# Nine gathers of the second layer placed between chunks made ahead, and the tokens' rows of h built before the top-k

## The chip, the cores and the metric

One core of a Trainium2 chip runs the whole program. The metric is the device time in microseconds, taken as the median of three runs: 3376.2 us before (3373.15 to 3382.22). One more execution was recorded by the hardware profiler; all rows below come from it.

## The reference

The program is two networks one after the other. The first has two layers, and each layer ends in a PEER block, a feed-forward layer with 16384 experts of which each token uses 8 heads times 16:

```python
q = (xc @ wq).reshape(C, PEER_HEADS, 2, PEER_KEY_DIM)
s = jnp.einsum('chpd,hpnd->chpn', q, sub_keys).astype(jnp.float32)
s1, i1 = lax.top_k(s[:, :, 0], PEER_TOPK)
s2, i2 = lax.top_k(s[:, :, 1], PEER_TOPK)
cand = (s1[..., :, None] + s2[..., None, :]).reshape(C, PEER_HEADS, PEER_TOPK * PEER_TOPK)
...
top, pos = lax.top_k(cand, PEER_TOPK)
eidx = jnp.take_along_axis(cidx, pos, axis=-1)
g = jax.nn.softmax(top, axis=-1).astype(xc.dtype)
a = jax.nn.gelu(jnp.einsum('chkd,cd->chk', u_tab[eidx], xc))
return jnp.einsum('chk,chkd->cd', g * a, v_tab[eidx])
```

The first layer's block runs over 512 tokens (latents and context), the second's over the 256 latents. The second network follows and is not touched.

## The kernel before

`peer` (from L707 on) computes the block in two ways at once. The first TD tokens (320 in the first layer, 192 in the second) go through all 16384 experts densely, in 128 chunks of 128 experts: TensorE multiplies the chunk's u rows (`peer_uT`) with h, ScalarE takes the gelu into a tile G (`expert_in`), VectorE multiplies G by the chunk's routing weights (A, L823), A is split into a high and a low part (Ahl, L128 and L129), and TensorE accumulates Ahl times the chunk's v rows (`peer_v`; lines L186 to L188 and L856, tiles ps). The remaining tokens, 64 in the second layer, are served by gathering: 64 indirect DMAs (L925, POOL's queue), each of which brings 128 pairs of u and v rows into a tile gat of 128 x 2048 floats, some 1.05 MB; there are four such tiles. For each gather VectorE multiplies u with the token's row of h and sums (L928), ScalarE applies gelu and the weight (L929, L930), and VectorE adds the weighted v row to gacc (L942; the first is L940). The gather of four places later can start when that has read its tile.

The order of one block is: norm and scores; the top-k of all heads on VectorE (`best`); `route`, which turns the result into indices (idx) for the gathers and into dense weights that POOL writes to DRAM (wd, L1065, twelve DMAs in the second layer); then the chunks made ahead, `AHEAD` of them (30 in the second layer, all with whole fp32 matmuls, L883, which need neither VectorE nor routing weights); then the main loop, which loads the routing weights of eight chunks at a time (win, L820, on POOL's queue, which reads wd) and runs chunk c's A while TensorE accumulates the v of chunk c - 3. From chunk 30 on the loop also makes its own u. The gathers are started by the generator `gathered`: each `next` issues one gather. In the first layer six are begun between the chunks made ahead (`if both and c % 2`), in the second none; the loop at L832 spreads the rest evenly over the chunks.

Before its first gather, `gathered` makes h2: the 64 tokens' rows of h, token by partition, by eight additions of the high and low part of h (hs, L919), eight transposes on TensorE (L920) and two copies (L921).

Instructions are put in order per engine by a scheduler at build time and run in that order on the chip: an instruction that waits holds all behind it on its engine, and a DMA that waits holds its queue. The loads of u and v (raw, L136) go over SP's queue into a ring of five tiles; each load starts when the tile five places earlier has been used. Up to four loads ahead are held split (whi, wlo).

Of the kernel before, what the change touches and what calls it, by code (L numbers as in the profile page):

```python
# [9 lines left out]
F32 = mybir.dt.float32  # L10
# [9 lines left out]
D = 1024  # L20
# [20 lines left out]
def bc(ap, shape):  # L41
    return ap.to_broadcast(shape)
# [6 lines left out]
class Net:  # L49
# [660 lines left out]
    def peer(self, l, both):  # L710


        nc, i = self.nc, self.i
        NT = 4 if both else 2
        T, TD = NT * 128, DENSE[l]
        nd, part = TD // 128, TD % 128
        assert part in (0, 64)
        ng = (T - TD) * 128 // 128
        xt, modT = self.xt, self.modT
        with ExitStack() as es:  # L720
            pa = self.pool(es, f"pa{l}")
            lp = self.pool(es, f"lp{l}")

            h2 = pa.tile([128, 8, 2, T], FR, name="h2hl")
            hT = h2[:, :, 0], h2[:, :, 1]
            h32 = None if both else pa.tile([128, 8, T], F32, name="h2f")
            sc = self.mod_scale(modT, 4, "nfT", l, pa)
            idx = pa.tile([128, max(ng, 1)], I32, name="idx")
            gg = pa.tile([128, max(ng, 1)], F32, name="gg")
# [12 lines left out]
            pos = [vp.tile([128, 8, 16], U32, name=f"pos{t}") for t in range(NT)]  # L742
            with ExitStack() as e2:
                np_ = self.pool(e2, "wqp", side="right")
                scs = {}

                def scores(cg):

                    qT = np_.tile([128, 4, 512], F32, tag="pq", name="pq", bufs=2)
                    keys = np_.tile([128, 4, 128], F32, tag="keys", name="keys", bufs=2)  # L750
                    nc.gpsimd.dma_start(keys, i["keysT"][l, cg])
                    for c in range(4):
                        ps = self.psum(c % 2)
                        self.proj_T(ps[:, :T], hT, i["wq"][l, cg * 4 + c], 0, T)
                        nc.scalar.copy(qT[:, c, :T], ps[:, :T])
                        yield
                    for t in range(NT):
                        ps = self.psum()
                        for k in range(4):
                            nc.tensor.matmul(ps[:, k * 128:k * 128 + 128], qT[:, k, t * 128:t * 128 + 128], keys[:, k],  # L760
                                             start=True, stop=True)
                        sc = scs[cg, t] = np_.tile([128, 512], F32, tag="score", name="score", bufs=8)
                        nc.scalar.copy(sc, ps)

                def best(cg):
                    for t in range(NT):
                        sc = scs[cg, t]
                        for c in range(4):
                            n = cg * 4 + c
                            self.top16(np_, sc[:, c * 128:c * 128 + 128], v16[t][:, n], i16[t][:, n], "tk")  # L770
                        self.candidates(np_, v16[t], top[t], pos[t], cg)


                made = [scores(cg) for cg in range(4)]
                for cg in range(5):
                    if cg < 4:
                        next(made[cg])
                    if cg:
                        for _ in made[cg - 1]:
                            pass  # L780
                    for _ in range(3 if cg < 4 else 0):
                        next(made[cg])
                    if cg and both:
                        best(cg - 1)
                if not both:
                    for cg in range(4):
                        best(cg)
            with ExitStack() as e2:
# [13 lines left out]
            ahead = AHEAD[l]  # L802
            em.close()
            gp = self.pool(es, f"gp{l}", side="right")
            gat = self.gathered(gp, hT, idx, gg, TD, T) if ng else iter(())

            gs, g0 = [], 0
            for c in range(ahead):
                gs.append(self.expert_in(lp, l, c, h2, h32, TD, c < WHOLE[l]))
                if both and c % 2:  # L810
                    next(gat, None)
                    g0 += 1
            acc = [[self.psum(t == 2 and n) for n in range(2)] for t in range(nd + bool(part))]
# [3 lines left out]
            for c in range(128):  # L817
# [4 lines left out]
                a = gp.tile([128, TD], F32, tag="A", name="A", bufs=2)  # L822
# [35 lines left out]
            for t in [*range(nd + bool(part), NT), *range(nd + bool(part))]:  # L858
                oo = gp.tile([128, 2, D], F32, tag="gat", name="gat", bufs=4)
                for n in range(2):  # L860
                    d = slice(n * 512, n * 512 + 512)
                    o, ps = oo[:, 0, d], acc[t][n] if t <= nd and t * 128 < TD else None
                    if t == nd and part:
                        self.evac(oo[:, 1, d], ps)
                        ps = self.psum()
# [35 lines left out]
        nc.scalar.activation(g, src, AF.Gelu_apprx_tanh)  # L901
        return g

    def gathered(self, gp, hT, idx, gg, t0, t1):


        nc, i = self.nc, self.i
        self.gacc = {}
        s0, prev = 0, None
        for t in reversed(range(t0 // 128, t1 // 128)):  # L910
            b = max(t0, t * 128)
            w = t * 128 + 128 - b
            h2 = gp.tile([128, D], F32, tag="h2", name="h2", bufs=1)
            for n in range(2):
                ps = self.psum(True)
                for k in range(4):
                    hs = gp.tile([128, 128 // w, w], F32, tag="hs", name="hs", bufs=2)
                    hh, hl = (bc(x[:, n * 4 + k, None, b:b + w].bitcast(F32), [128, 128 // w, w]) for x in hT)
                    nc.vector.tensor_add(hs, hh, hl)  # L919
                    nc.tensor.transpose(ps[:, k * 128:k * 128 + 128], hs.rearrange("p a b -> p (a b)"), self.ident)  # L920
                nc.scalar.copy(h2[:, n * 512:n * 512 + 512], ps)  # L921
            acc = self.gacc[t] = gp.tile([128, D], F32, tag="gacc", name="gacc", bufs=2)
            for s in range(s0, s0 + w):
                uv = gp.tile([128, 2, D], F32, tag="gat", name="gat", bufs=4)
                nc.gpsimd.indirect_dma_start(out=uv.rearrange("p a b -> p (a b)"), out_offset=None, in_=i["peer_uv"],  # L925
                                             in_offset=bass.IndirectOffsetOnAxis(ap=idx[:, s:s + 1], axis=0))
                a = gp.tile([128, 2], F32, tag="pga", name="pga", bufs=4)
                nc.vector.scalar_tensor_tensor(uv[:, 0], uv[:, 0], 1.0, h2, op0=OP.mult, op1=OP.mult, accum_out=a[:, 0:1])  # L928
                nc.scalar.activation(a[:, 1:2], a[:, 0:1], AF.Gelu_apprx_tanh)  # L929
                nc.scalar.activation(a[:, 1:2], a[:, 1:2], AF.Copy, scale=gg[:, s:s + 1])  # L930
                if prev:
                    self.gather_add(*prev)
                prev = acc, uv, a, s == s0
                yield
            s0 += w
        self.gather_add(*prev)
# [784 lines left out]
```

## Time and profile before

| | |
|---|---|
| median of the timed runs | 3376.2 us |
| profiled execution, its own time | 3371.84 us |
| its span | 3370.1 us |
| PE busy | 3230.3 us (96%) |
| DVE busy | 2607.3 us (77%) |
| ACT busy | 1748.3 us (52%) |
| POOL busy | 519.6 us (15%) |
| DMA | 860.52 MB, mean 255 GB/s |

The time of the profiled execution is 1.7 us over its span, and 4.4 us under the median of the timed runs. PE being busy 96% of the span is a mean over many stages. The second layer's PEER block takes the stretch from about 1957 to 2700 us; its top-k and routing lie between 1982 and 2146 us, and its main loop from 2161 us on.

### The profile page before, as it was taken

The page shows a single profiled execution, that of the slowest core. Times are in us where ns is not written, and L with a number is a line of the kernel's source. Part 1 is how long each engine was busy: PE and PEld are TensorE (multiplying, and loading weights), DVE is VectorE, ACT ScalarE, POOL GpSimd, SP SyncE. Part 2 cuts the span into 40 slices and gives each one's busy share as a digit, 9 for nine tenths or more (in the row PEclk, how much of TensorE's full clock was granted, in tenths as well). Part 3 has the DMA queues.
Part 4 walks back from the last instruction along what each step waited for, and adds up shares of the span by engine and source line. Part 5 has one row for each costly group of instructions (what it writes and reads, how often), then busy time and mean ns, then how long its engine had stood idle before and what let it go on. Part 6 is the DMA issues. An engine that isn't in the chain of part 4 may idle for free. (4 is left out here: it accounts for less than half of the span.)

```text
span 3370.1 us, 53059 instructions
## 1 busy us (share of the span) xinstructions
PE 3230.3 (96%) x19449; PEld 2775.4 (82%) x19449; DVE 2607.3 (77%) x5430; ACT 1748.3 (52%) x3720; POOL 519.6 (15%) x432
## 2 busy tenths in 40 slices
PE   8999999879899999999999997989999999999998
PEld 5666788758788989888877997769999988889887
DVE  3643449998899999999966678599999968756875
ACT  3443332385455555554545544557777755555554
POOL 0000000113333333333300000122222100000000
PEclk9999999879999999999999998999999999999999
DMA  6566232569999999999944555889999854255432
GB/s 243 187 213 225 85 125 83 167 185 345 375 400 391 387 388 388 380 393 386 377 166 163 179 179 174 286 347 384 367 377 377 336 173 157 94 185 177 137 126 107
DMA packets 196453, 860.52 MB, mean 255 GB/s; under 512 B 23920, under 2 KB 25664, under 8 KB 159712
## 3 DMA queue, kind: packets, MB, share of 16 engines
q1 hardware_dynamic: 141840, 505.94, 41.6%
q0 software_dynamic: 54352, 351.20, 27.1%
q8 instruction: 153, 2.51, 0.3%
q14 instruction: 108, 0.88, 0.1%
HBM read 816.15 MB, written 40.89 MB: 254 GB/s over the span
## 5 line engine op out<-in xcount | busy, mean ns | idle before, releaser
L129 DVE TENSOR_TENSOR wlo<-raw,whi 128x1024 fp32r<-128x1024 f32 x778 | 943.9, 1221 | 392.7 <-ACT whi L128 379.9
L128 ACT CAST whi<-raw 128x1024 fp32r<-128x1024 f32 x778 | 815.8, 1049 | 627.2 <-PE pf L187 247.4
L925 POOL DMA_INDIRECT gat<-peer_uv,idx x256 | 413.8, 1616 | 918.8 <-DVE gacc L942 875.2
L188 PE MATMUL pf<-h2hl,wlo 128*128 128x320 f32 (+2 forms) x1152 | 361.9, 314 | 7.6 <-DVE wlo L129 7.6
L186 PE MATMUL pf<-h2hl,whi 128*128 128x320 f32 (+2 forms) x1152 | 362.7, 315 | 0.2 <-ACT mo L321 0.2
L187 PE MATMUL pf<-h2hl,whi 128*128 128x320 f32 (+2 forms) x1152 | 361.8, 314 | 0.0
L928 DVE SCALAR_TENSOR_TENSOR gat<-gat,h 128x1024 f32<-128x1024 f32 x256 | 312.1, 1219 | 32.5 <-DMA gat<-peer_uv,idx 31.2
L942 DVE SCALAR_TENSOR_TENSOR gacc<-gat,pga,gacc 128x1024 f32<-128x1024 f32 x253 | 323.5, 1279 | 0.0
L187 PE MATMUL ps<-wlo,Ahl 128*128 128x512 f32 x768 | 305.4, 398 | 10.5 <-DVE wlo L129 10.4
L186 PE MATMUL ps<-whi,Ahl 128*128 128x512 f32 x768 | 302.3, 397 | 2.8 <-ACT Ahl L128 2.8
L188 PE MATMUL ps<-whi,Ahl 128*128 128x512 f32 x768 | 303.4, 395 | 0.5 <-DVE Ahl L129 0.5
L892 PE MATMUL pf<-h2hl,whi 128*128 128x384 f32 x784 | 238.3, 359 | 4.6 <-ACT whi L128 4.3
L188 PEld LDWEIGHTS pf<-h2hl,wlo 128*128 128x128 f32 x1152 | 217.9, 189 | 11.6 <-DVE wlo L129 8.8
L187 PEld LDWEIGHTS pf<-h2hl,whi 128*128 128x128 f32 x1152 | 218.2, 189 | 8.0
L186 PEld LDWEIGHTS pf<-h2hl,whi 128*128 128x128 f32 x1152 | 218.2, 189 | 7.8 <-ACT mo L321 0.3
L128 ACT CAST Ahl<-A 128x320 fp32r<-128x320 f32 (+1 forms) x256 | 103.7, 405 | 164.2 <-DVE A L823 158.0
L187 PEld LDWEIGHTS ps<-wlo,Ahl 128*128 128x128 f32 x768 | 145.0, 189 | 37.5 <-DVE wlo L129 14.0
L891 PE MATMUL pf<-h2hl,wlo 128*128 128x192 f32 x686 | 174.9, 255 | 0.0
L188 PEld LDWEIGHTS ps<-whi,Ahl 128*128 128x128 f32 x768 | 145.3, 189 | 34.9 <-DVE Ahl L129 1.0
L186 PEld LDWEIGHTS ps<-whi,Ahl 128*128 128x128 f32 x768 | 145.0, 189 | 28.6 <-ACT Ahl L128 4.1
L892 PEld LDWEIGHTS pf<-h2hl,whi 128*128 128x128 f32 x784 | 147.5, 188 | 9.4 <-ACT whi L128 5.2
L856 PE MATMUL ps<-wlo,Ahl 128*128 128x512 f32 x384 | 151.4, 397 | 0.0
(613 smaller groups left out, 7574.7 us busy)
## 6 DMA issues: line engine op xcount, KB each, us to landing
raw<-peer_uT SPq DMA_DIRECT2D x256, 512.0 KB
raw<-peer_v SPq DMA_DIRECT2D x256, 512.0 KB
raw<-ada_w SPq DMA_DIRECT2D x96, 512.0 KB
wd<-wb POOLq DMA_DIRECT2D x32, 1024.0 KB
raw<-w_g SPq DMA_DIRECT2D x48, 512.0 KB
win<-wd POOLq DMA_DIRECT2D x16, 1280.0 KB
raw<-wq SPq DMA_DIRECT2D x32, 512.0 KB
raw<-w2o SPq DMA_DIRECT2D x32, 512.0 KB
```

What stands on the lines that cost most here:

```text
L128: nc.scalar.copy(hi, src)
L129: nc.vector.tensor_sub(lo, src, hi.bitcast(F32))
L186: mm(ps, ah, bh, start=start, stop=False)
L187: mm(ps, ah, bl, start=False, stop=False)
L188: self.last = mm(ps, al, bh, start=False, stop=stop).ins
L856: nc.tensor.matmul(acc[nd][n], ahl[:, 2 * TD - part:], v[e][:, n], start=b == 0 and e == 0, stop=b == 127 and e == 1)
L891: mm(src, u[1][:, k], h2[:, k, 0, :TD], start=False, stop=False)
L892: self.last = mm(r3(ps[:, :2 * TD], 2), u[0][:, k], h2[:, k, :, :TD], start=k == 0, stop=k == 7).ins
L925: nc.gpsimd.indirect_dma_start(out=uv.rearrange("p a b -> p (a b)"), out_offset=None, in_=i["peer_uv"], in_offset=bass.IndirectOffsetOnAxi ...
L928: nc.vector.scalar_tensor_tensor(uv[:, 0], uv[:, 0], 1.0, h2, op0=OP.mult, op1=OP.mult, accum_out=a[:, 0:1])
L942: self.nc.vector.scalar_tensor_tensor(acc, uv[:, 1], a[:, 1:2], acc, op0=OP.mult, op1=OP.add)
```

## The change

Three edits, all in the PEER block of the second layer:

- The code that makes h2 becomes a function `by_token`, which the second layer calls before `best`, in the pool lp. `gathered` takes the ready tile. The first layer still makes it inside `gathered`.
- Between the chunks made ahead, `gathered` is now also stepped in the second layer, after chunks 13, 15, ... 29: nine gathers.
- With nine done, the loop spreads 55 gathers over its chunks instead of 64, by the same rule.

```diff
@@ peer @@
                 np_ = self.pool(e2, "wqp", side="right")
-                scs = {}
+                scs, h2s = {}, {}
...
                 if not both:
+                    h2s[nd] = self.by_token(lp, hT, TD, part)
                     for cg in range(4):
                         best(cg)
...
-            gat = self.gathered(gp, hT, idx, gg, TD, T) if ng else iter(())
+            gat = self.gathered(gp, hT, idx, gg, TD, T, h2s) if ng else iter(())
...
                 gs.append(self.expert_in(lp, l, c, h2, h32, TD, c < WHOLE[l]))
-                if both and c % 2:
+                if c % 2 and (both or c > 11):
                     next(gat, None)
                     g0 += 1
@@ new, with the body that stood in gathered @@
+    def by_token(self, gp, hT, b, w):
+        nc = self.nc
+        h2 = gp.tile([128, D], F32, tag="h2", name="h2", bufs=1)
+        for n in range(2):
+            ps = self.psum(True)
+            for k in range(4):
+                hs = gp.tile([128, 128 // w, w], F32, tag="hs", name="hs", bufs=2)
+                hh, hl = (bc(x[:, n * 4 + k, None, b:b + w].bitcast(F32), [128, 128 // w, w]) for x in hT)
+                nc.vector.tensor_add(hs, hh, hl)
+                nc.tensor.transpose(ps[:, k * 128:k * 128 + 128], hs.rearrange("p a b -> p (a b)"), self.ident)
+            nc.scalar.copy(h2[:, n * 512:n * 512 + 512], ps)
+        return h2
@@ gathered @@
-    def gathered(self, gp, hT, idx, gg, t0, t1):
+    def gathered(self, gp, hT, idx, gg, t0, t1, h2s={}):
...
-            h2 = gp.tile([128, D], F32, tag="h2", name="h2", bufs=1)
...
+            h2 = h2s.get(t) or self.by_token(gp, hT, b, w)
```

Where the instructions stand. POOL's queue in the second layer, from the last write of the routing weights (wd1 from wb) on; win are loads of routing weights for the main loop, gat the gathers. Before:

```order
L1065 DMA wd1_19185<-wb_21245 128x16x128
L820 DMA win_21710<-wd1_19185 128x1536
L925 DMA gat_21854<-peer_uv,idx_19183 128x2048
L820 DMA win_21876<-wd1_19185 128x1536
L925 DMA gat_21906<-peer_uv,idx_19183 128x2048
L925 DMA gat_21957<-peer_uv,idx_19183 128x2048
L925 DMA gat_22008<-peer_uv,idx_19183 128x2048
L820 DMA win_22082<-wd1_19185 128x1536
```

The first load of routing weights follows the last write at once. The same place on POOL after the change, where the line numbers are seven higher for the gathers and one higher for win:

```order
L1072 DMA wd1_19185<-wb_21274 128x16x128
L932 DMA gat_21528<-peer_uv,idx_19183 128x2048
L932 DMA gat_21560<-peer_uv,idx_19183 128x2048
L932 DMA gat_21593<-peer_uv,idx_19183 128x2048
L932 DMA gat_21626<-peer_uv,idx_19183 128x2048
L932 DMA gat_21659<-peer_uv,idx_19183 128x2048
L932 DMA gat_21692<-peer_uv,idx_19183 128x2048
L932 DMA gat_21725<-peer_uv,idx_19183 128x2048
L932 DMA gat_21758<-peer_uv,idx_19183 128x2048
L932 DMA gat_21791<-peer_uv,idx_19183 128x2048
L821 DMA win_21802<-wd1_19185 128x1536
L821 DMA win_21932<-wd1_19185 128x1536
```

All nine gathers now stand ahead of the first win, and five of them reuse a gat tile that VectorE has to read first.

DVE between the end of the routing (ol is its last tile) and the first multiplications of the main loop (A). Before:

```order
L1056 TENSOR_TENSOR ol_21281<-o2_21279,gl_21039 128x512
L823 TENSOR_TENSOR A_21712<-G_21327,win_21710 128x192
L823 TENSOR_TENSOR A_21718<-G_21340,win_21710 128x192
L129 TENSOR_TENSOR Ahl_21714<-A_21712,Ahl_21714 128x192
L823 TENSOR_TENSOR A_21724<-G_21353,win_21710 128x192
L129 TENSOR_TENSOR Ahl_21720<-A_21718,Ahl_21720 128x192
```

The first A comes right behind the routing. After the change, DVE from the fourth gather's product (L935, formerly L928) to the first A:

```order
L935 SCALAR_TENSOR_TENSOR gat_21626,pga_21628<-gat_21626,h2_19875 128x1024
L129 TENSOR_TENSOR wlo_21831<-raw_21828,whi_21830 128x1024
L949 SCALAR_TENSOR_TENSOR gacc_21527<-gat_21626,pga_21628,gacc_21527 128x1024
L935 SCALAR_TENSOR_TENSOR gat_21659,pga_21661<-gat_21659,h2_19875 128x1024
L949 SCALAR_TENSOR_TENSOR gacc_21527<-gat_21659,pga_21661,gacc_21527 128x1024
L935 SCALAR_TENSOR_TENSOR gat_21692,pga_21694<-gat_21692,h2_19875 128x1024
L949 SCALAR_TENSOR_TENSOR gacc_21527<-gat_21692,pga_21694,gacc_21527 128x1024
L935 SCALAR_TENSOR_TENSOR gat_21725,pga_21727<-gat_21725,h2_19875 128x1024
L949 SCALAR_TENSOR_TENSOR gacc_21527<-gat_21725,pga_21727,gacc_21527 128x1024
L935 SCALAR_TENSOR_TENSOR gat_21758,pga_21760<-gat_21758,h2_19875 128x1024
L935 SCALAR_TENSOR_TENSOR gat_21791,pga_21793<-gat_21791,h2_19875 128x1024
L824 TENSOR_TENSOR A_21804<-G_21356,win_21802 128x192
```

DVE has nine products and eight sums of gathers (the first three pairs stand above this piece) between the routing and the first A, and one split of a v tile (wlo).

DVE inside the top-k, where six of the eight additions of by_token now stand (L914, formerly L919); tk, v16 and i16 belong to the top-k of one head. After the change:

```order
L958 MAX v16_0_19189<-tk_20072 128x8
L914 TENSOR_TENSOR hs_19883<-h2hl_19174 128x128
L914 TENSOR_TENSOR hs_19886<-h2hl_19174 128x128
L959 MAX_INDEX i16_0_19191<-v16_0_19189,tk_20072 128x8
L914 TENSOR_TENSOR hs_19891<-h2hl_19174 128x128
L914 TENSOR_TENSOR hs_19894<-h2hl_19174 128x128
L956 MAX_INDEX i16_0_19191<-v16_0_19189,score_19756 128x8
L914 TENSOR_TENSOR hs_19897<-h2hl_19174 128x128
L957 MATCH_REPLACE tk_20078<-v16_0_19189,score_19756 128x128
L914 TENSOR_TENSOR hs_19900<-h2hl_19174 128x128
```

The other two stand earlier, beside the norm; before, all eight stood in the main loop among the first chunks. On TensorE the eight transposes now stand between the scores and the second chunk made ahead.

## Rows read from the trace of the kernel before

**Rows 1.** Busy us by stretch: PE, PEld, DVE, ACT, POOL, clock, DMA, GB/s
```profile
2042.40:2056.00 13.60, 3.36 (x20) 2.90 (x19) 13.53 (x92) 0.37 (x2) 0.00 (x0) 0.69 0.13 44
...
2161.00:2172.60 11.60, 9.73 (x51) 9.46 (x49) 4.33 (x11) 4.16 (x14) 0.00 (x0) 0.85 1.02 422
2172.60:2213.00 40.40, 40.28 (x180) 32.36 (x178) 34.96 (x62) 25.14 (x55) 7.88 (x6) 1.00 0.90 348
2213.00:2250.00 37.00, 25.76 (x98) 18.57 (x97) 31.22 (x47) 17.82 (x45) 10.27 (x7) 0.95 0.88 342
2250.00:2280.00 30.00, 28.65 (x159) 25.32 (x160) 28.44 (x43) 18.43 (x43) 7.29 (x5) 1.00 0.93 358
2280.00:2680.00 400.00, 400.00 (x2263) 363.73 (x2262) 384.65 (x579) 288.23 (x621) 82.98 (x56) 1.00 0.95 375
```

**Rows 2.** The same view for L856 alone (PE busy, times it ran)
```profile
2172.60:2250.00 77.40, 30.10 (x106) 20.12 (x106) 0.98 0.89 345
```

**Rows 3.** Timeline of PE: start us, us, engine, line, operation, tiles
```profile
2163.14 9.75 PE L883 MATMUL pf<-h2f,raw 128*128 128x192 f32 x48 [1.87 <-ACT G L901]
2172.59 0.53 PE L186 MATMUL ps<-whi,Ahl 128*128 128x512 f32 x1
```

**Rows 4.** Timeline of PE after its long wait
```profile
2059.98 0.95 PE L883 MATMUL pf<-h2f,raw 128*128 128x192 f32 x2
...
2063.22 0.54 PE L883 MATMUL pf<-h2f,raw 128*128 128x192 f32 x2
```

**Rows 5.** Timeline of POOL, second layer: what ended its wait in brackets
```profile
2145.53 1.15 POOL L1065 DMA_DIRECT2D wd<-wb  x1 [3.25 <-ACT G L901]
2153.11 0.56 POOL L820 DMA_DIRECT2D win<-wd  x1 [6.43 <-DMA wd<-wb]
2153.98 1.01 POOL L925 DMA_INDIRECT gat<-peer_uv,idx  x1 [0.30 <-issue]
```

**Rows 6.** Timeline of DVE, second layer, start of the main loop
```profile
2160.88 0.63 DVE L823 TENSOR_TENSOR A<-G,win 128x192 f32<-128x192 f32 x2 [18.86 <-DMA win<-wd]
2161.65 0.36 DVE L129 TENSOR_TENSOR Ahl<-A,Ahl 128x192 fp32r<-128x192 f32 x1
```

**Rows 7.** Timeline of POOL, first layer, the same place
```profile
779.89 1.07 POOL L925 DMA_INDIRECT gat<-peer_uv,idx  x1 [3.87 <-PE pf L920]
...
794.00 1.67 POOL L925 DMA_INDIRECT gat<-peer_uv,idx  x1 [1.92 <-DVE gacc L942]
795.68 0.61 POOL L820 DMA_DIRECT2D win<-wd  x1
```

**Rows 8.** Timeline of DVE, first layer, the same place
```profile
778.93 0.48 DVE L919 TENSOR_TENSOR hs<-h2hl 128x128 f32<-128x128 f32 x2
...
781.98 0.30 DVE L919 TENSOR_TENSOR hs<-h2hl 128x128 f32<-128x128 f32 x1 [0.19 <-PE pf L920]
786.80 1.23 DVE L928 SCALAR_TENSOR_TENSOR gat<-gat,h 128x1024 f32<-128x1024 f32 x1 [4.52 <-DMA gat<-peer_uv,idx]
...
803.51 1.23 DVE L928 SCALAR_TENSOR_TENSOR gat<-gat,h 128x1024 f32<-128x1024 f32 x1
...
809.15 0.89 DVE L823 TENSOR_TENSOR A<-G,win 128x320 f32<-128x320 f32 x2 [1.98 <-DMA win<-wd]
```

**Rows 9.** Timeline of ACT: the first expert load of the main loop arrives
```profile
2168.52 1.04 ACT L128 CAST whi<-raw 128x1024 fp32r<-128x1024 f32 x1 [4.33 <-DMA raw<-peer_v]
```

**Rows 10.** Timeline of SP's DMA queue: the same load's issue opens this row
```profile
2158.70 69.44 SPq L136 DMA_DIRECT2D raw<-peer_v  x24
```

**Rows 11.** DVE's groups by line, 2172.6 to 2280 us
```profile
L129 DVE TENSOR_TENSOR wlo<-raw,whi 128x1024 fp32r<-128x1024 f32 x36 | 43.8, 1220 | 6.1 <-ACT whi L128 6.0
L928 DVE SCALAR_TENSOR_TENSOR gat<-gat,h 128x1024 f32<-128x1024 f32 x15 | 18.3, 1220 | 0.0
L942 DVE SCALAR_TENSOR_TENSOR gacc<-gat,pga,gacc 128x1024 f32<-128x1024 f32 x13 | 16.6, 1279 | 0.0
...
L919 DVE TENSOR_TENSOR hs<-h2hl 128x128 f32<-128x128 f32 x8 | 2.0, 286 | 0.1
```

More of the change, by code (lines that the diff above doesn't have):

```diff
@@ L912, in gathered @@
             w = t * 128 + 128 - b
-            h2 = gp.tile([128, D], F32, tag="h2", name="h2", bufs=1)
[L914 to L921, printed above, removed]
+            h2 = h2s.get(t) or self.by_token(gp, hT, b, w)
             acc = self.gacc[t] = gp.tile([128, D], F32, tag="gacc", name="gacc", bufs=2)
```

## The prediction

> **What bounds the kernel now.** I read the busy time by stretch first, because the 96% of PE is a mean. [rows 1] cut the second layer's PEER block at the places where the pattern changes. From 2280 us on PE is busy 400.00 of 400.00 us: nothing that eases DMA or DVE there can be worth anything. Three stretches before it are not full. From 2042.4 to 2056 PE has 3.36 busy us in 13.6 while DVE works 13.53: PE waits for the top-k. From 2172.6 to 2250 PE loses 0.12 and then 11.24 us, with DMA at 0.88 to 0.90 and DVE busy 34.96 + 31.22 = 66.2 of 77.4 us; from 2250 to 2280 it loses another 1.35. So 12.7 us of PE time are lost between the start of the main loop and its steady part, and that is all that lighter DMA or DVE work there can return.
>
> Then I read when the main loop starts and why. On PE the chunks made ahead end and the first v product starts at 2172.59 [rows 3]. DVE's first A had been done since 2160.88, after a wait of 18.86 us for win [rows 6]; win was issued at 2153.11, when the last write of wd had landed [rows 5]. The start of the main loop therefore has 2172.59 - 2162.0 = 10.6 us of slack against its routing weights (2162.0 is the end of the first Ahl, 1.1 us after A began). A change that delays the first A by more than this delays PE.
>
> **The change part by part.**
>
> *h2 ahead of the top-k.* The eight additions cost 2.0 us in the main loop [rows 11]. Six of them now stand in the top-k, which ends in the wait of PE at 2042 to 2056: 6/8 of 2.0 is 1.5 us, and every step of route behind it moves by that. With the round trips to PE for the two hs tiles it can be more: in the first layer the chain of eight runs from 778.93 to 782.3, 3.4 us [rows 8]. I take 1.6 (0 if some later wait absorbs it, 3.4 at most). The eight transposes and two copies lie on PE and ACT, beside the 10 us in which PE has nothing to do; if that cover were gone they would cost about a us.
>
> *Nine gathers ahead of the first win.* POOL runs in order. The last wd is issued at 2145.53 + 1.6 = 2147.1, the first gather 1.15 us later, at 2148.3. The second seems to need what the first win needed before, the landing of wd (2153.11 + 1.6). From the fifth on each waits for a gat tile, so for a product and a sum on DVE, and win waits behind the ninth. DVE, too, has all nine products ahead of the first A, so the first A can't slip by. ACT has gelus of the gathers between the last G of the chunks made ahead, which hold PE's tiles pf; the last G stands behind the fifth gather's, and even at 5 us a gather that is 2148.3 + 6.9 + 4 x 5 + 1.2 = 2176.4, well ahead of A, so I count nothing for it. On SP's queue no load changes its place.
>
> The trace has this very pattern once, with six gathers, in the first layer: first gather issued at 779.89, the sixth at 794.00, win at 795.68 [rows 7], the first product at 786.80, the sixth at 803.51, the first A at 809.15 [rows 8]. From first gather to first A that is 29.3 us, and a gather takes (803.51 - 786.80)/5 = 3.34 us. Three more make 39.3 us, and the first A of the second layer starts at 2148.3 + 39.3 = 2187.6, instead of 2160.88.
>
> Both ends of this. Early: all of DMA's 422 GB/s [rows 1] (2161 to 2172.6) goes to the gathers, 1.05 MB in 2.5 us each. The ninth lands 6.9 us (first layer, 779.89 to 786.80) + 8 x 2.5 after 2148.3, its issue ends some 5 us sooner, and win needs 7.8 us from issue to A (2153.11 to 2160.88): A at 2177.8. Late: SP's loads take half, as the v load did that was issued at 2158.70 [rows 10] and reached ACT at 2168.52 [rows 9], 9.8 us for 0.52 MB among four gathers. Then 9 x 5.0 = 45 us, and a product of 1.2: A at 2194.5. I take 2187.6, the row of the same pattern.
>
> The rows put one gather alone at 6.9 us and one in a stream at 3.34. The Trainium skill's "DMA: Bandwidth & Descriptors", section "Anatomy of one DMA — SWDGE (gpsimd) path", has it cheaper: about 2.0 us plus bytes over 436 GB/s, by estimate 4.4 us for a gather alone and 2.4 in a stream. By it A would come near the early end, and the sum would be about 10 us less. The same page, section "Queues, rings and completion order", speaks against the change: each DMA engine goes round between the queues that have work, so gathers share evenly with SP's loads, and A would come at the late end. The 9.8 us of the v load agree with that one.
>
> *PE's wait.* The first v product follows A by 1.1 us: 2188.7, which is 16.1 us after 2172.59. The chunks made ahead don't fill this: they end where they did, since nothing was added to them. Behind it stand all the v products. After its wait PE also starts slowly: after 2056 two u products took 0.95 us at first and 0.54 us later [rows 4], and the granted clock was 0.69 in the stretch before, between the two levels of 1.2 and 2.4 GHz [rows 1]. Some four us at half speed are 2 us; a part may be hidden, so 1.5 (0 to 2).
>
> *What comes back.* The rule of the loop gives 25 x 64 // 119 = 13 gathers by chunk 30 before and 25 x 55 // 119 = 11 now: the nine done ahead thin the rest out evenly, they don't clear the stretch that is short. PE did 106/4 = 26.5 v chunks from 2172.6 to 2250 [rows 2], so this is the stretch in question. DVE saves there two gathers of 1.2 + 1.3 us, 5.0, and hs of 2.0; DMA saves 2 x 1.05 MB, at the 345 GB/s of that stretch 6.1 us. DVE's other work stays, of which the 36 splits alone are 43.8 us [rows 11]. I take 6 of the 12.7 us (0 if the order of the waits doesn't change, 12.7 if all are returned). From 2280 us on PE is full, so seven fewer gathers there return nothing, and nothing later can catch up.
>
> *The sum.* 16.1 + 1.5 - 6 = 11.6 us later, on the profiled execution's 3371.84: 3383.4. The median of the runs is 3376.2, 4.4 above that execution, so 3388.
>
> **The rivals.**
>
> *No change that can be told.* Some 0.3% (10.1 us) is what a measurement of this kernel can tell from none. If A comes at 2181 (+9.5 for PE with its 1.1) and 8 to 9 us of lost time return, the two cancel: 3376 to 3378. For it: the second layer's gathers have no splits of u beside them on DVE, as the first layer's have. Against it: the chunks made ahead still draw 0.52 MB each over SP.
>
> *Faster.* The gathers pass at the full 422 GB/s, A starts at 2177.8 and PE at 2178.9, 6.3 us late; with DMA and DVE ahead of PE from then on all 12.7 us return, less the wait for the clock: -6.4, so 3370. It decides if A comes before 2184.2 and the stretch from 2172.6 to 2250 becomes full on PE. Against it: 11 of 13 gathers are still in that stretch.
>
> *A larger loss.* The even sharing holds, A at 2194.5, PE 23.0 late, 2 for the clock and only 4 back: +21, 3397. For it speaks the v load's 9.8 us.
>
> *The change doesn't begin the gathers earlier.* All nine wait for wd's landing because the gat tiles lie where route's tiles lay. Then the chain starts at 2154.7 instead of 2148.3 and A comes at 2194; with 6 back that is +18 to +19, 3395.
>
> **How the numbers follow.** Forecast (A from 2184 to 2192, 4 to 8 us returned, 3382 to 3394): 0.48, of which 0.36 lies over 3386.3. No change: 0.25. Faster: 0.09; its own sum stays within 0.3%, so 0.03 of it counts as same, and 0.06 stand for a gain that no row shows. Larger loss 0.15, not earlier 0.03. Slower by over 0.3% is 0.36 + 0.15 + 0.03 = 0.54, within is 0.12 + 0.25 + 0.03 = 0.40, faster 0.06. All lower ends together (-1.6 and -9.8 on A, no clock, all 12.7 back) give -8, all upper ends +26; the range 3371 to 3399 leaves out those corners and somewhat under 2 in 10.
>
> **What would show it.** On POOL: gathers right behind the last wd, the first win some 30 us after it. On DVE: nine products in the idle time of 2142 to 2161 and on, and the first A at about 2187. On PE: 10 to 20 us without work between the last L883 and the first L186 of tile ps, then a stretch of 26 chunks with about half of the 11 us lost there, then the same 400 full us. If the gap on PE is under 8 us, or if PE is full from the first v product on, the forecast is wrong; if the top-k or route ends more than 3 us later, the first term is.

## The result, and the profile after

The changed kernel takes 3397.36 us (median of six runs, 3393.95 to 3404.5) against 3373.88 for the kernel before on the same chip: ratio 1.0069, interval 1.0058 to 1.0079, 23.3 us slower. Its profiled execution took 3396.31 us (span 3394.5), that of before 3371.84 (span 3370.1): the two traces differ by 24.4 us, all of it in the second layer's block.

The same stretches as in [rows 1], after (PE, PEld, DVE, ACT, POOL, clock, DMA, GB/s):

```profile
2042.40:2056.00 13.60, 11.18 (x69) 10.88 (x67) 13.53 (x96) 1.32 (x4) 0.00 (x0) 1.00 0.56 198
...
2161.00:2172.60 11.60, 10.69 (x66) 10.34 (x66) 6.27 (x8) 1.76 (x7) 2.03 (x3) 1.00 1.02 422
2172.60:2213.00 40.40, 21.99 (x91) 17.92 (x91) 29.40 (x47) 16.64 (x45) 13.05 (x9) 0.75 0.93 364
2213.00:2250.00 37.00, 32.09 (x134) 24.35 (x133) 31.55 (x51) 19.16 (x44) 10.64 (x7) 1.00 0.91 339
2250.00:2280.00 30.00, 21.84 (x94) 15.88 (x92) 25.42 (x40) 15.80 (x38) 7.43 (x6) 1.00 0.88 329
2280.00:2680.00 400.00, 399.97 (x2240) 361.04 (x2241) 368.26 (x552) 280.80 (x597) 72.49 (x51) 1.00 0.91 354
```

Four stretches changed. From 2042.4 to 2056 PE works 11.18 instead of 3.36 us, because it now waits earlier: 5.37 us for hs inside the top-k, and then 3.2 instead of 10.2 us for the first tile of the routing (pr). From 2172.6 to 2213 it works 21.99 of 40.4 instead of 40.28; that is the new wait. From 2213 to 2250 it loses 4.91 us instead of 11.24, from 2250 to 2280 8.16 instead of 1.35: about as much in all (13.1 against 12.6), but later. From 2280 on both are full, and DVE and DMA have more room (368 instead of 385 busy, 354 instead of 375 GB/s) that nothing uses.

POOL's timeline after, which answers to [rows 5]: start, us, then what ended its wait.

```profile
2146.17 1.15 POOL L1072 DMA_DIRECT2D wd<-wb  x1 [3.41 <-ACT G L902]
2147.63 1.01 POOL L932 DMA_INDIRECT gat<-peer_uv,idx  x1 [0.30 <-issue]
2153.68 0.99 POOL L932 DMA_INDIRECT gat<-peer_uv,idx  x1 [5.04 <-PE pf L884]
...
2160.23 0.94 POOL L932 DMA_INDIRECT gat<-peer_uv,idx  x1 [3.08 <-DVE gacc L947]
...
2179.76 1.68 POOL L932 DMA_INDIRECT gat<-peer_uv,idx  x1 [8.71 <-DVE gacc L949]
2182.79 1.68 POOL L932 DMA_INDIRECT gat<-peer_uv,idx  x1 [1.35 <-DVE gacc L949]
2184.47 1.17 POOL L821 DMA_DIRECT2D win<-wd  x2
```

The first gather follows the last wd, the ninth is issued at 2182.79, and the first two win behind it at 2184.47, 31.4 us after the 2153.11 of before. The ninth had waited, as the four before it, for a sum of DVE (gacc) to free its tile; the wait of 8.71 us ahead of the eighth is the longest. The second was issued 7.5 us after the last wd, as win was before (7.6 us); that it, too, waited for wd's landing is likely but not shown, since the profile names a u product as what released it.

DVE's timeline shows where that came from:

```profile
2157.32 1.23 DVE L935 SCALAR_TENSOR_TENSOR gat<-gat,h 128x1024 f32<-128x1024 f32 x1 [14.97 <-DMA gat<-peer_uv,idx]
...
2170.39 1.23 DVE L935 SCALAR_TENSOR_TENSOR gat<-gat,h 128x1024 f32<-128x1024 f32 x1 [0.54 <-DMA gat<-peer_uv,idx]
...
2177.07 1.23 DVE L129 TENSOR_TENSOR wlo<-raw,whi 128x1024 fp32r<-128x1024 f32 x1 [5.45 <-ACT whi L128]
2178.21 1.28 DVE L949 SCALAR_TENSOR_TENSOR gacc<-gat,pga,gacc 128x1024 f32<-128x1024 f32 x1
2179.41 1.22 DVE L935 SCALAR_TENSOR_TENSOR gat<-gat,h 128x1024 f32<-128x1024 f32 x1
...
2191.51 1.22 DVE L935 SCALAR_TENSOR_TENSOR gat<-gat,h 128x1024 f32<-128x1024 f32 x1
...
2192.68 0.63 DVE L824 TENSOR_TENSOR A<-G,win 128x192 f32<-128x192 f32 x2
```

The first product starts at 2157.32. After the fourth (2170.39) stands a split of a v tile, wlo, which DVE reaches at 2171.6 and can begin only at 2177.07. What it waits for is the first v load of the main loop, on SP's queue (the load's issue opens the row) and on ACT:

```profile
2163.61 91.82 SPq L136 DMA_DIRECT2D raw<-peer_v  x24
```

```profile
2175.99 1.04 ACT L128 CAST whi<-raw 128x1024 fp32r<-128x1024 f32 x1 [7.25 <-DMA raw<-peer_v]
2176.95 0.20 ACT L936 ACTIVATE pga<-pga 128x1 f32<-128x1 f32 x1
```

The load is issued at 2163.61 and reaches ACT 12.4 us later, among the gathers (9.8 us before, [rows 9, 10]). Until then the gelu of the fourth gather (pga) stands behind the cast on ACT, and its sum behind the split on DVE. With that stall the first A comes at 2192.68 and not at 2160.88 [rows 6].

PE, as in [rows 3]:

```profile
2172.35 2.84 PE L884 MATMUL pf<-h2f,raw 128*128 128x192 f32 x16 [0.92 <-DMA raw<-peer_uT]
2193.60 0.80 PE L186 MATMUL ps<-whi,Ahl 128*128 128x512 f32 x1 [18.41 <-ACT Ahl L128]
2194.19 0.63 PE L187 MATMUL ps<-wlo,Ahl 128*128 128x512 f32 x1
...
2198.18 0.40 PE L187 MATMUL ps<-wlo,Ahl 128*128 128x512 f32 x1
```

The chunks made ahead end 2.3 us later than before (2172.35 + 2.84 = 2175.19 against 2163.14 + 9.75 = 2172.89, [rows 3]), and PE then waits 18.41 us. Its first products are 0.43 us apart, from 2198.18 on 0.23: ten of them after the wait, with the granted clock at 0.54 of full speed between 2193.60 and 2198.18 (near the lower of its two levels, 1.2 GHz) and at 1.00 after; that costs 2.0 us. The last v product of the main loop, before and after (PE, the same columns):

```profile
2714.59 0.39 PE L856 MATMUL ps<-wlo,Ahl 128*128 128x512 f32 x1
```

```profile
2740.00 0.40 PE L857 MATMUL ps<-wlo,Ahl 128*128 128x512 f32 x1
```

So the first v product is 21.0 us later (2193.60 against 2172.59) and the last 25.4: 4.4 us are lost on the way, 2.0 of them by the clock. Nothing came back.

### The profile page after: what moved, and what is told of

Its sections match the earlier page's. It is cut to its first block, busy times and chain, and to the rows that moved or that the text cites. A ratio compares the mean times of both kernels' runs of the same rounds, so it can differ in the third digit from the quotient of the medians.

```text
span 3394.5 us, 53067 instructions
## 1 busy us (share of the span) xinstructions
PE 3234.9 (95%) x19449; PEld 2775.5 (82%) x19449; DVE 2611.1 (77%) x5430; ACT 1747.2 (51%) x3720; POOL 519.5 (15%) x432
## 4 chain that ended last, share of the span: by engine, by line
PE 68%; issue 15%; DVE 9%; DMA 5%; ACT 2%; POOL 1%; SPq 0%; DVEq 0%; POOLq 0%; ACTq 0%
PE pf L188 8%; PE pf L186 8%; PE pf L187 8%; PE ps L187 7%; PE ps L188 7%; PE ps L186 7%; PE pf L893 4%; PE ps L857 4%; PE pf L892 2%; DVE wlo L129 2%; PE pf L370 2%; DMA gat<-peer_uv,idx 2%; DMA wd<-wb 1%; PE pf L857 1%; DMA raw<-peer_v 1%
## 5 line engine op out<-in xcount | busy, mean ns | idle before, releaser
L935 DVE SCALAR_TENSOR_TENSOR gat<-gat,h 128x1024 f32<-128x1024 f32 x256 | 312.8, 1222 | 59.0 <-DMA gat<-peer_uv,idx 57.3
L186 PE MATMUL ps<-whi,Ahl 128*128 128x512 f32 x768 | 302.5, 397 | 24.1 <-ACT Ahl L128 24.0
L187 PE MATMUL ps<-wlo,Ahl 128*128 128x512 f32 x768 | 305.3, 398 | 6.4 <-DVE wlo L129 6.4
L188 PE MATMUL ps<-whi,Ahl 128*128 128x512 f32 x768 | 304.4, 396 | 0.5 <-DVE Ahl L129 0.5
L187 PEld LDWEIGHTS pf<-h2hl,whi 128*128 128x128 f32 x1152 | 218.3, 189 | 7.9
L186 PEld LDWEIGHTS pf<-h2hl,whi 128*128 128x128 f32 x1152 | 218.4, 190 | 7.5
L936 ACT ACTIVATE pga<-pga 128x1 f32<-128x1 f32 x256 | 51.5, 201 | 207.6 <-DVE gat L935 207.6
L857 PE MATMUL ps<-whi,Ahl 128*128 128x512 f32 x384 | 151.4, 397 | 0.0
```

The lines of the kernel that those rows point to most:

```text
L186: mm(ps, ah, bh, start=start, stop=False)
L187: mm(ps, ah, bl, start=False, stop=False)
L188: self.last = mm(ps, al, bh, start=False, stop=stop).ins
L857: nc.tensor.matmul(acc[nd][n], ahl[:, 2 * TD - part:], v[e][:, n], start=b == 0 and e == 0, stop=b == 127 and e == 1)
```

## The experiments

Theory W is that of the prediction: the gathers hold back the first A, and PE waits for it. Rival H: h2 in the top-k delays everything. Rival B: what counts is how many gathers, with their bytes, lie ahead of the steady part. Later a rival D was added, that VectorE's work for them counts. Ratios are of the timed runs to those of the kernel before in the same set; "loop" is the time on PE from the first v product to the last, from each kernel's profiled execution. The times of the first A and the first v hold a shift of up to 7.7 us that was there before the block (the last section); the loop does not. "By chunk 30" counts the gathers begun when chunk 30 has had its turn, those ahead of the loop included; from chunk 30 on the loop also makes its own u, and some chunks later PE is full.

| kernel | ahead | by chunk 30 | ratio (interval) | first A | first v | loop |
|---|---|---|---|---|---|---|
| before | 0 | 13 | 1 | 2160.88 | 2172.59 | 542.0 |
| changed | 9 | 20 | 1.0069 (1.0058 to 1.0079) | 2192.68 | 2193.60 | 546.4 |
| e1, h2 only | 0 | 13 | 0.9997 (0.9987 to 1.0007) | 2162.28 | 2178.77 | 541.7 |
| e2, gathers only | 9 | 20 | 1.0069 (1.0056 to 1.0082) | 2191.94 | 2200.25 | 542.8 |
| e3, four ahead | 4 | 16 | 1.0026 (1.0015 to 1.0038) | 2182.18 | 2182.97 | 543.6 |
| e4, win first | 9 | 20 | 1.0055 (1.0042 to 1.0068) | 2159.46 | 2174.85 | 562.0 |
| e5, pause | 9 | 13 | 1.0034 (1.0021 to 1.0047) | 2196.18 | 2197.12 | 531.2 |
| e6, win first and pause | 9 | 13 | 1.0004 (0.9995 to 1.0014) | 2161.43 | 2176.88 | 540.1 |
| e7, seven more | 0 | 20 | 1.0060 (1.0047 to 1.0072) | 2166.18 | 2176.93 | 563.5 |
| e8, begun later | 0 | 8 | 0.9980 (0.9971 to 0.9989) | 2158.68 | 2170.35 | 536.3 |
| e9, half bytes | 0 | 20 | 1.0017 (1.0007 to 1.0026) | 2162.32 | 2172.35 | 551.4 |
| e10, no sums | 0 | 20 | 1.0039 (1.0025 to 1.0053) | 2166.83 | 2177.89 | 555.8 |
| e11, h2 and few early | 0 | 7 | 0.9954 (0.9941 to 0.9968) | 2158.59 | 2175.88 | 524.0 |
| e12, few early | 0 | 7 | 0.9939 (0.9926 to 0.9953) | 2165.44 | 2175.73 | 528.9 |

**Each half of the change alone.** e1 keeps by_token ahead of the top-k and no early gathers:

```diff
-                if c % 2 and (both or c > 11):
+                if c % 2 and both:
```

> h2 is made before the top-k, but no gather is begun between the chunks made ahead (64 are spread over the main loop, as before). Theory W (the nine gathers hold back the first load of routing weights and the first A, and TensorE waits for that; the move of h2 costs nothing): last write of wd under 1 us later than before, first A at 2161 to 2162, 3371 to 3377 us, ratio to before 0.999 to 1.001. Theory H (the eight additions and transposes in the top-k delay the routing and with it everything): first A 3 us or more late, ratio 1.003 or more. Theory B (the bytes of the gathers delay the loads of u and v): as W.

No change (0.9997), though the last wd was 4.3 us later in its profiled execution (2149.82): 3.5 of them were there already at the norm that opens the block (its reciprocal, L240, at 1961.24 instead of 1957.78). e2 has the nine gathers and leaves h2 in the generator (the line with h2s[nd] is taken out):

> Nine gathers between the chunks made ahead, but h2 is made where it was, inside the generator, just ahead of the first gather. Theories W and B: as the changed kernel, first A at 2190 to 2195, ratio to before 1.006 to 1.008. Theory H: without the additions in the top-k most of the loss goes, ratio under 1.003.

The whole loss (1.0069). H is out. e2's trace adds a point: there gathers' gelus stand ahead of more G on ACT, and PE's last two chunks made ahead (32 products) begin only at 2195.08, after A.

```profile
2195.08 5.47 PE L883 MATMUL pf<-h2f,raw 128*128 128x192 f32 x32 [1.33 <-ACT G L901]
```

**Fewer, and in another order.** e3 begins four gathers ahead (`c > 21`):

> h2 before the top-k and four gathers ahead (after chunks 23, 25, 27, 29) instead of nine, so that none waits for a gat tile before the first load of routing weights; 60 in the main loop. Theory W: that load is issued near 2158, the first A comes at 2170 to 2176 (four products and one split of a v tile stand ahead of it), TensorE starts on v 0 to 4 us late, ratio 0.999 to 1.002. Theory B: the loss goes by bytes, 4/9 of 23 us, ratio about 1.003.

A came at 2182.18, not by 2176, in part for the same reason as above: the split of a v tile behind the fourth product waited 5.48 us. The whole block also ran late in this execution, by 5.7 us already at the norm (1963.49). The ratio, 1.0026, is near the one that B expected, but with A this late W would give a loss as well, and its upper end, 1.002, lies in the interval: e3 does not separate the two. e4 issues the first win ahead of the gathers; the loop then uses this tile for its first eight chunks (not shown):

```diff
             for c in range(ahead):
+                if not both and c == 13:
+                    win0 = gp.tile([128, TD // 16, 8, 16], F32, tag="win", name="win", bufs=2)
+                    dma0 = nc.gpsimd.dma_start(win0.rearrange("p b c t -> p (b c t)"), wd[0])
```

> The same nine gathers at the same place, but the first load of routing weights is issued ahead of them; with it the first five A stand ahead of all products on VectorE. Theory W: first A at 2161 to 2162, TensorE's wait of 18.4 us before its first v product goes, at most 8 us of the loss stay: ratio 1.0025 or less. Theory B: the loads of u and v are as late as with the change, 15 us or more stay: ratio 1.0045 or more, with TensorE waiting for loads from 2172 on.

This spoke against W as the whole cause. PE's wait of 18.4 us is gone and yet four fifths of the loss stay (1.0055, 18.6 us). The loop is 562.0 us long instead of 542.0. DMA is full in its first 40 us (415 and 417 GB/s, a share of 1.02; before 0.90 and 348 GB/s, [rows 1]), and PE waits elsewhere, time and again, for splits (the views of stretches and of PE's timeline):

```profile
2172.60:2193.60 21.00, 16.06 (x65) 12.57 (x64) 15.28 (x20) 8.92 (x24) 7.31 (x5) 0.87 1.02 415
2193.60:2213.00 19.40, 16.04 (x56) 11.41 (x55) 15.46 (x25) 8.41 (x21) 5.77 (x5) 0.88 1.02 417
```

```profile
2185.52 0.51 PE L186 MATMUL ps<-whi,Ahl 128*128 128x512 f32 x1 [1.05 <-ACT Ahl L128]
2187.93 0.62 PE L187 MATMUL ps<-wlo,Ahl 128*128 128x512 f32 x1 [1.91 <-DVE wlo L129]
...
2203.99 0.50 PE L187 MATMUL ps<-wlo,Ahl 128*128 128x512 f32 x1 [0.76 <-DVE wlo L129]
```

**The count ahead of the steady part.** e5 and e6 are the changed kernel and e4 with a pause, so that by chunk 30 no more gathers are begun than before; the order ahead of A stays. Here and below only the rule for the second layer is shown; the first layer keeps its own:

```diff
-                while done < min(g0 + max(c - c0, 0) * (ng - g0) // (124 - c0), ng):
+                while done < min(max(g0, max(c - c0, 0) * ng // (124 - c0)), ng):
```

> The changed kernel, but after its nine early gathers no more are begun until the rule of before (64 spread over the whole loop) has caught up with nine, near chunk 22, so that 13 are begun by chunk 30, as before, instead of 20. The order ahead of the first A is the changed kernel's. Theory B (what counts is how many gathers' bytes lie ahead of the steady part: 1.05 MB at 420 GB/s is 2.5 us each, seven more are 17.5 us; the late A adds only some 5 us): most of the 23 us go, ratio 1.0005 to 1.003, and TensorE is full once its first v product has started. Theory W (the late A is the cost, 21 us of wait and 2 us at the lower clock, and nothing is returned): ratio 1.0055 to 1.0075.

> The same pause, with the first load of routing weights ahead of the nine gathers. Theory B: neither more bytes than before nor a late A: ratio 0.998 to 1.002. Theory W in the form that is left after the second trial (the waits behind the gathers on VectorE and the late v load): as there, 1.004 to 1.006.

e5 loses half (1.0034, a little more than B's 1.003): its first v product is as late as the change's (2197.12), and its loop is 10.8 us shorter than before's. W's lowest value, 1.0055, is outside its interval. e6 loses nothing (1.0004). Then the opposite, with no gather ahead at all; e7 begins 20 instead of 13 gathers between chunks 5 and 30, e8 eight:

```diff
+ e7: max(c - c0, 0) * 20 // 25 if c < 30 else min(20 + (c - 30) * 44 // 94, ng)
+ e8: c0 = 16 instead of 5, the rule unchanged
```

> The kernel before, with no gather ahead of the main loop, but 20 instead of 13 gathers begun between chunks 5 and 30, the other 44 spread over the rest. The first A comes at 2161 as before. Theory B: seven more gathers ahead of the steady part cost 2.5 us each, 17 us, ratio 1.004 to 1.006. Theory W: no loss without a late A, ratio under 1.002.

> The kernel before with its gathers begun from chunk 16 on instead of chunk 5: 8 by chunk 30 instead of 13. Theory B: five gathers fewer ahead of the steady part give back 2.5 us each, at most the 12.7 us that TensorE loses there; faster by 6 to 12 us, ratio 0.9965 to 0.998, unless VectorE, busy 96% in the steady part, becomes its bound with 0.59 gathers per chunk instead of 0.54: then 1.000 to 1.003, with TensorE no longer full between 2280 and 2680 us. Theory W says nothing on it: 1.000.

Both as B has them, at the edge of its ranges. e7 alone gives nearly the loss of the change (1.0060, some 20 us of 3375, 2.9 for each of the seven), with the routing weights in time; e8 is 6.5 us faster than before.

**Bytes or VectorE.** In the changed kernel, from 2253.55 us on, there is a cycle of two chunks and one gather, on DVE without a gap:

```profile
2256.36 0.35 DVE L129 TENSOR_TENSOR Ahl<-A,Ahl 128x192 fp32r<-128x192 f32 x1
2256.63 0.35 DVE L824 TENSOR_TENSOR A<-G,win 128x192 f32<-128x192 f32 x1
2256.90 1.22 DVE L935 SCALAR_TENSOR_TENSOR gat<-gat,h 128x1024 f32<-128x1024 f32 x1
...
2258.04 0.36 DVE L129 TENSOR_TENSOR Ahl<-A,Ahl 128x192 fp32r<-128x192 f32 x1
2258.32 1.28 DVE L949 SCALAR_TENSOR_TENSOR gacc<-gat,pga,gacc 128x1024 f32<-128x1024 f32 x1
2259.51 1.22 DVE L129 TENSOR_TENSOR wlo<-raw,whi 128x1024 fp32r<-128x1024 f32 x1
2260.65 0.35 DVE L824 TENSOR_TENSOR A<-G,win 128x192 f32<-128x192 f32 x1
2260.92 1.22 DVE L129 TENSOR_TENSOR wlo<-raw,whi 128x1024 fp32r<-128x1024 f32 x1
2262.05 0.35 DVE L129 TENSOR_TENSOR Ahl<-A,Ahl 128x192 fp32r<-128x192 f32 x1
```

From the first Ahl of this piece to the last are 5.69 us, and from one of PE's waits for wlo to the next as well, where PE's own twenty products of two chunks take 4.67 (20 x 0.2333, the pace after 2198.18):

```profile
2260.78 0.50 PE L187 MATMUL ps<-wlo,Ahl 128*128 128x512 f32 x1 [0.76 <-DVE wlo L129]
...
2266.47 0.50 PE L187 MATMUL ps<-wlo,Ahl 128*128 128x512 f32 x1 [0.59 <-DVE wlo L129]
```

That made theory D, that VectorE bounds this part. It does not hold for the whole stretch: DVE is busy 31.55 of 37 and 25.42 of 30 us there, and between 2213 and 2280 us it waits 10.0 us in all for ACT's half of Ahl. The last of these waits, 2.5 us up to 2253.55, follows a cast that stood on ACT for a v load:

```profile
2252.22 1.04 ACT L128 CAST whi<-raw 128x1024 fp32r<-128x1024 f32 x1 [4.02 <-DMA raw<-peer_v]
```

To part the two, e9 halves the bytes of e7's first 20 gathers and e10 leaves out all but one of their sums, so neither computes the block's values any more:

```diff
+ e9:  in_ = peer_uv.rearrange("r (t d) -> (r t) d", t=2), into uv[:, 0] alone, for s < 20
+ e10: gather_add skipped for 2 <= s <= 20
```

> As the kernel with seven more gathers in the main loop (ratio 1.006), but the first 20 gathers fetch rows of half the length (128 x 1024, 0.52 MB; other rows, and the u part serves as v part too), with every operation of VectorE, ScalarE and TensorE and their order as there. Theory B (DMA's bytes are what costs): 20 x 0.52 = 10.5 MB less, at 420 GB/s 25 us, the loss goes: ratio 0.996 to 1.001. Theory D (VectorE is the bound of the stretch: in the changed kernel two chunks and one gather take it 5.69 us, TensorE needs 4.66): ratio 1.005 to 1.007, TensorE's waits for wlo as there (16.8 us).

> As the kernel with seven more gathers in the main loop, but of the first 20 gathers VectorE adds only the first weighted row to gacc; 19 sums are left out, the gathers are whole. Theory D: 19 x 1.19 = 22.6 us less on VectorE, the loss of 20 us goes: ratio 0.997 to 1.001, with DMA as busy as there. Theory B: the bytes are the same, ratio 1.005 to 1.007.

Neither theory is the whole: each cut removes a part. Half the bytes take the ratio from 1.0060 to 1.0017 (14.5 us), no sums to 1.0039 (7.1 us). D misses both by more than the intervals. B misses both narrowly: its nearest values, 1.001 and 1.005, lie inside them. The intervals of e7 and e10 overlap a little, so VectorE's part is the smaller and by the times alone the less certain one. The loops say the same (563.5 us in e7, 551.4 in e9, 555.8 in e10), and what is left in the traces shows the other limit. The same stretch in e7, e9 and e10, with ACT's wait for v loads (2172 to 2280 us; total, times, longest) behind each:

```profile
2213.00:2250.00 37.00, 25.51 (x94) 17.50 (x93) 32.72 (x50) 14.90 (x40) 12.71 (x9) 0.95 0.95 358
```

```profile
ACT whi L128 <- DMA raw<-peer_v: 30.3, 12, 7.0
```

```profile
2213.00:2250.00 37.00, 26.58 (x106) 19.30 (x107) 37.00 (x57) 18.98 (x48) 15.68 (x11) 1.00 0.84 300
```

```profile
ACT whi L128 <- DMA raw<-peer_v: 12.2, 7, 2.8
```

```profile
2213.00:2250.00 37.00, 25.53 (x91) 17.56 (x89) 23.13 (x40) 16.45 (x41) 10.64 (x8) 0.93 1.01 409
```

```profile
ACT whi L128 <- DMA raw<-peer_v: 37.7, 14, 7.5
```

With half the bytes DVE is busy 37.00 of 37.00 us and ACT waits 12.2 us for v; without the sums DMA's share is 1.01 and ACT waits 37.7. So a gather uses up two things that are both short here: some 2.5 us of DMA (1.05 MB at 422 GB/s) and 1.22 + 1.28 us of VectorE. How much of the loss falls to each in the changed kernel itself was not tried; these cuts were made in e7's order.

**A version that is faster than both.** e11 is e1, and e12 the kernel before, with 7 gathers between chunks 3 and 30 and 57 after:

```diff
+ max(c - 3, 0) * 7 // 27 if c < 30 else min(7 + (c - 30) * 57 // 94, ng)
```

> h2 before the top-k, no gather ahead of the main loop, and 7 gathers instead of 13 begun between chunks 3 and 30, the other 57 spread over the last 98. By either theory the stretch before 2280 us becomes full for TensorE: six gathers fewer by 2.3 us and more each, at most the 12.7 us that were lost there: faster by 6 to 12 us, ratio 0.9965 to 0.998. If VectorE becomes the bound of the steady part (57/94 = 0.61 gathers per chunk, its busy share 0.96 at 0.54): 0.999 to 1.002.

> The kernel before with the pace of the faster kernel (7 gathers between chunks 3 and 30, 57 after), h2 made inside the generator in the main loop, as before. If the pace alone gives the gain: ratio 0.9945 to 0.9965, as there (0.9954). If making h2 ahead of the top-k has a part in it, now that VectorE and DMA have room (TensorE waited 2.5 us for hs in the kernel that began at chunk 16): 0.997 to 0.9985, and TensorE waits 2 us and more for hs near chunk 7.

0.9954 (3359.3 us) and 0.9939 (3357.8 us): 0.46 and 0.61%, or 16 and 21 us, faster, somewhat more than was expected of either. h2 ahead has no part in it that could be told: the intervals overlap, and in e12 PE's wait for hs is 1.0 us. The stretches of e11, as above:

```profile
2172.60:2213.00 40.40, 39.66 (x178) 33.08 (x179) 33.04 (x55) 25.67 (x58) 6.18 (x5) 1.00 0.89 336
2213.00:2250.00 37.00, 37.00 (x181) 31.57 (x180) 34.94 (x55) 24.85 (x54) 8.28 (x6) 1.00 0.94 359
2250.00:2280.00 30.00, 30.00 (x170) 27.19 (x169) 28.86 (x44) 21.28 (x47) 6.60 (x4) 1.00 0.98 386
2280.00:2680.00 400.00, 400.00 (x2269) 363.90 (x2268) 395.49 (x593) 286.91 (x628) 89.81 (x61) 1.00 0.98 382
```

PE is full from 2213 on. The steady part takes the extra gathers, DVE at 395 of 400 us, and PE stays at 400.00. e11's loop is 18.0 us shorter, more than the 12.7 us that the busy time of before shows as lost. The v products done by 2280 us tell it better (L856 before and L857 in e11 alone, four to a chunk: PE, PEld, clock, DMA, GB/s):

```profile
2172.60:2280.00 107.40, 36.41 (x130) 24.66 (x131) 0.98 0.90 348
```

```profile
2172.60:2280.00 107.40, 38.87 (x144) 27.05 (x144) 1.00 0.94 358
```

That is 3.5 chunks more, though e11 began 3.3 us later; a chunk of the steady part takes 4.6 us (400 us for 349 such products before). By estimate some 19 us are gained there, so the busy time of PE hid a part of what was lost.

## Why the prediction was right, and where it was not

**h2 ahead of the top-k** was taken at +1.6 us. The last wd is 0.6 us later (2146.17 against 2145.53); counted from the block's norm it is 0.7 us later, in e1 0.8 later and in e11 1.2 earlier, and e1 is no slower. So the term was small, as taken, and its 1.6 us were too many; that PE would wait 5.37 us for hs was not foreseen, and cost nothing that can be told, since PE waited that much less behind it.

**Nine gathers ahead of the first win.** The place and the order were as read: gathers behind the last wd, win behind the ninth, A behind the ninth product, the second gather at 2153.68, about where win had waited for wd's landing (2153.11, [rows 5]). A was taken at 2187.6 and came at 2192.68. The first layer's pattern has no split of a v tile between its products; this one has, as the order showed, and I gave it no price. DVE stood there 5.45 us. That the rest adds up is partly luck: up to the fourth product the gathers took some 6 us more than in the first layer (9.7 instead of 6.9 us from the first issue to the first product, then 4.36 instead of 3.34 a gather), and from the fifth product to A some 6 us less (3.03 a gather, and 1.17 instead of 5.64 us from the last product to A). That the loads share DMA with the gathers was a rival's reason for a late A; here it acted on the first gathers and through this one load. The 12.4 us of the load agree with sharing, which the Trainium skill describes in "DMA: Bandwidth & Descriptors", section "Queues, rings and completion order"; that the shares are even, as I concluded from it, no run here shows. What the Trainium skill gives in "DMA: Bandwidth & Descriptors", section "Anatomy of one DMA — SWDGE (gpsimd) path", by my estimate 4.4 us for a gather alone, could not be tested: DMA's share was 1.00 from 2148 to 2154 us, and nor was the 6.9 us of the first layer that of a gather alone (0.94 from 780 to 787 us).

**PE's wait** was taken at 16.1 and 1.5 for the clock; measured 21.0 and 2.0. The mechanism was right, its size short by the split that I had left out.

**What comes back** is the step that failed. I took 6 of 12.7 us back, because the main loop has 11 instead of 13 gathers by chunk 30. PE lost 13.1 us again between 2193.6 and 2280 (0.75 to 2230, 4.2 to 2250, 8.2 after), and the loop became 4.4 us longer. I had counted the gathers in the stretch, but not those ahead of it that use the same DMA and the same DVE: 20 instead of 13 now lie ahead of the steady part. These seven cost some 20 us with no gather ahead of the loop (e7 against before), 17 with nine ahead and A early (e4 against e6), and 12 with A late (the changed kernel against e5). So the late A hides about a third of their cost, since the loads catch up while PE waits. The late A alone costs some 12 us (e5), of 24.5 us that its first v product is late (3.5 of them from before the block): there the return that I had forecast did come, and the loop is 10.8 us shorter. The forecast's sum, a late A and a return, thus fits e5; for the changed kernel it had the right sign and half the size (11.6 against 23.3). The four kernels with nine gathers ahead show how the two overlap: both causes 1.0069, without the late A 1.0055, without the seven 1.0034, without both 1.0004. The ceiling of 12.7 us was wrong too: e12 gained 21 us (interval 16 to 25) with the pace alone.

**The rivals.** The sum of "a larger loss" (A at 2194.5, PE 23.0 late, 4 back), 3397, is the measured time, which lies 3 us above the band that I had thought likeliest (3382 to 3394); its A and its wait of PE were nearly right, its 4 us back were not, and neither was even sharing shown to be the reason. "No change" needed A at 2181 and 8 to 9 us back; neither came. "The change doesn't begin the gathers earlier" is out by POOL's rows. "Faster" asked that the stretch get full on PE; e11 shows that it can, by taking gathers out of it. In the range, all upper ends together come to +26.8 and not +26; nothing else hung on that.

## What to carry to other kernels

Before work is moved ahead of a stretch that waits for loads, count what lies ahead of the point from which the bound engine is full: bytes and VectorE time of the whole, not of the stretch alone. None of the six kernels here that began gathers in the idle time in front was faster, not even e6, which kept the count and had A early. Where a later part has the bound engine full and the others still have room, the work belongs there: here 6 gathers moved to it gave 16 to 21 us, and 7 moved the other way cost 20 (e7).

## What the runs showed that was not expected

- The last wd was issued between 2145.4 and 2153.0 us in these executions (2145.53 before, 2152.95 in e10). Nearly all of that was there before the block: the reciprocal of its norm (L240) came at 1957.78 before and at 1965.48 in e10, and from it to the last wd are 186.5 to 188.6 us in every kernel but e2 (183.6). So it comes from ahead of every edit; why, was not looked for. Spans and start times of single executions therefore carry some 7 us that have nothing to do with an edit behind it; the length of the loop on PE does not.
- In the second layer's stretches of 10 us and more that were read here, DMA moved at most 422 GB/s (422 before, after and in e4, 421 in e11, all from 2161 to 2172.6 us). That is the figure to count bytes by, not the mean of 345 in a stretch where PE also waits.
- VectorE at 395 of 400 us beside a full PE (e11) cost PE nothing.
